# A two-layer hybrid decoder trunk on one core: the first projections in a written order, the levels of a triangular inverse ahead of their bank's readers, and one buffer taken later

## The chip, the core and the metric

The kernel runs on one core of a Trainium2 chip. The metric is device time in microseconds (us) of one execution, the median of three runs. TensorE (PE in the profile) multiplies matrices into PSUM banks of 128 partitions by 512 float32 values; VectorE (DVE), ScalarE (ACT) and GpSimd (POOL) do the rest, and all DMAs here are issued by SyncE (SP).

## The reference

Two pre-norm residual layers over 1,024 tokens of width 1,024, float32. Layer 0 has a gated DeltaNet and a short gated convolution side by side, layer 1 an HGRN2 recurrence and a dilated window attention; each layer ends with a SwiGLU feed-forward of 2,816 hidden columns. The parts that the change touches:

```python
hn = rms_norm(h, norm_mix_g[layer])
qkv, z, beta_raw, alpha_raw, gate_b, gate_c, sc_in = split_cols(h @ w_in, AB_SPLITS)
qkv = silu(causal_depthwise_conv(qkv, conv_w))          # width 4
...
# gated delta rule, chunks of tokens, one triangular solve per chunk and head
sol = triangular_solve(a_strict + eye(c), rhs, lower=True, unit_diagonal=True)
...
return (silu(h @ w_gate) * (h @ w_up)) @ w_down         # swiglu
```

## The kernel before

Tokens are held transposed: features on the partitions, tokens along the free dimension, in two halves of 512. A tile of x is 128 features by 512 tokens; there are 8 of them (d = 0 to 7) for each half. To keep float32 accuracy at the fast matmul rate, every operand is split into a rounded high part and the remainder (`split`, L97: a copy on ScalarE, L99, and a subtraction on VectorE, L100), and `mm3` (L120) makes each product of three matmuls: high by high (L123), low by high (L124) and high by low (L125). `proj` (L131) runs 8 such triples into one PSUM bank: 24 matmuls for 128 output columns and 512 tokens.

PSUM has three groups of banks: `psu` (3 buffers), `psm` (3) and `psg` (2). A new tile of a group waits for the readers of the tile that had the buffer before it.

Most of the program's order on each engine is made by a scheduler that looks at priorities and expected times. Inside `manual_schedule` the engines named keep the order in which the code records the work.

*The start.* x is loaded by SP together with the first four weights, `("ab", 0)`, `("ab", 4)`, `("ab", 8)`, `("ab", 12)` (query, key, value and gate of head 0; 512 KB each, two staging buffers `raw`). For each half and each d, ScalarE makes the high part of x times the gain (L1655), VectorE the low part (L1656), and `Trunk.piece` (L169) squares x on ScalarE and adds the squares up on VectorE (L183). `Trunk.rms` (L185) sums over the partitions with small matmuls (L195), VectorE adds epsilon (L198) and GpSimd takes the power (L200); `Trunk.spread` (L204) broadcasts the result over the partitions with matmuls (L209), and ScalarE copies it to `rb` (L1659). The projections are of the unscaled x: `rb` is multiplied in afterwards, where VectorE reads the bank (L781 in `conv_silu`, L721 in `z_gate`). All of this is left to the scheduler.

*Units.* `mixer_ab` goes through 8 units u: head h = u // 2 and half u % 2. A unit is four projections (query, key, value, gate), the convolution of width 4 over the first three (`conv_silu`: L781, L790, L792, then a Tanh on ScalarE and L796), and `z_gate`. Between them, `step` (L862) runs pieces of other work by the letters of `plan` (L858): S is a piece of `scalars` (beta and decay), A and B are the two parts of `chunk_mats` of earlier units.

*The inverse.* After a substitution on blocks of 32, `delta` builds the inverse of each chunk's 128 by 128 triangle in levels. `level1` and `level2` make the off-diagonal blocks of 32, `level3` and `level4` those of 64. Each level is a few small matmuls into a part of a `psg` bank, and then a read of it: level1 by VectorE (L975), level2 by VectorE (L990), level3 by ScalarE (L1002), level4 by VectorE (L1009). In one tick level4 of chunk c + 1 and level2 of chunk c + 2 share a bank, in the next one level3 and level1. TensorE's order here is written out: `short_conv`'s projections are cut in halves of 12 matmuls, and a tick of `delta` stands between them.

*The turn of the feed-forward.* `Up` multiplies with a Strassen-like scheme: the products are named p1 to p7, and `Up.turn` (L410) writes out the order for the first three weight columns while the second half's operands are made. `rest` (L463) makes low parts of operands (L413) from `tr.h`, the trunk's tiles; then `close()` frees these tiles, and the pool `self.right` is opened over their memory. `take` (L266) gives a weight buffer: the 9th and 10th taken are the first ones that lie in this pool. `p7` (L359) copies its bank out to `c` (L362, ScalarE), which for f = 0 is also a tile of this pool (`kept`, L349), and adds z to it (L363); `end` (L368) goes on accumulating into the same bank after that copy.

## Time and profile before

| | us |
|---|---|
| median of 3 runs (lowest to highest) | 2687.57 (2687.46 to 2688.88) |
| the profiled execution, by the same clock as the runs | 2687.8 |
| its span, from the first instruction to the last | 2686.0 |

The profiled execution thus has 1.8 us around its span, and lies 0.2 us above the median of the runs. Times in the trace count from the start of the span. In a row of the timeline stand start, duration, engine, line, operation, tiles and the number of instructions merged (x8); brackets give how long the engine had been idle before it, and what ended that. Matmuls overlap, so the start of one to the start of the next is less than the duration shown.

### The profile page before, as it was taken

The numbers are of one execution on the slowest core, as the hardware profiler recorded it, in microseconds if no ns is written. First come the engines' busy times: TensorE is split into PE (matmuls) and PEld (weight loads), VectorE is DVE, ScalarE is ACT, GpSimd is POOL, SyncE is SP. The second block draws the span as 40 slices with busy tenths as digits, with TensorE's granted clock in tenths as the row PEclk, the third lists the DMA queues.
The fourth block names the chain that finished last, engine by engine and source line by source line (L and its number), as shares of the span: only waits on it lengthen the run. The fifth ranks groups of instructions, "written<-read, shape, count | busy, mean of one in ns | idle before, by whom it ended". The sixth has DMA issues, their size and how long they took to land.

```text
span 2686.0 us, 36890 instructions
## 1 busy us (share of the span) xinstructions
PE 2654.1 (99%) x14604; PEld 2221.7 (83%) x14604; DVE 1479.6 (55%) x2463; ACT 986.0 (37%) x1623; POOL 480.4 (18%) x434
## 2 busy tenths in 40 slices
PE   8999999999999999999999999999999999999998
PEld 6888788878888888888888888888887888888887
DVE  7887676583434443345665557477658344444342
ACT  4432123343333332323444345354434333333232
POOL 0110121334333201010000000000034343320100
PEclk9999999999999999999999999999999999999999
DMA  3424346422222384441222322323742222237342
GB/s 131 141 96 165 108 140 208 146 75 90 84 81 81 99 274 129 154 131 52 79 67 73 87 64 68 99 64 123 241 147 75 91 86 81 91 101 262 114 137 94
DMA packets 166285, 310.65 MB, mean 116 GB/s; under 512 B 26048, under 2 KB 65504, under 8 KB 165984
## 3 DMA queue, kind: packets, MB, share of 16 engines
q1 hardware_dynamic: 166112, 308.30, 35.3%
q8 instruction: 114, 1.87, 0.3%
q14 instruction: 59, 0.48, 0.1%
HBM read 234.22 MB, written 74.01 MB: 115 GB/s over the span
## 4 chain that ended last, share of the span: by engine, by line
PE 94%; DVE 3%; issue 1%; DMA 1%; ACT 1%; POOL 0%; SPq 0%; POOLq 0%; DVEq 0%; ACTq 0%
PE psu L123 20%; PE psu L125 20%; PE psu L124 20%; PE psg L123 5%; PE psg L125 5%; PE psg L124 5%; PE psm L123 3%; PE psm L124 3%; PE psm L125 3%; PE psm L1487 1%; PE psm L1461 1%; PE psg L1250 1%; PE psm L195 1%; PE psm L1476 1%; DVE h L413 1%
## 5 line engine op out<-in xcount | busy, mean ns | idle before, releaser
L100 DVE TENSOR_TENSOR w<-raw,w 128x1024 fp32r<-128x1024 f32 (+1 forms) x324 | 404.8, 1251 | 442.5 <-ACT w L99 441.2
L99 ACT CAST w<-raw 128x1024 fp32r<-128x1024 f32 (+1 forms) x324 | 319.5, 987 | 635.2 <-PE psg L125 230.8
L123 PE MATMUL psu<-hnh,w 128*128 128x512 f32 x1328 | 530.2, 399 | 6.9 <-ACT w L99 6.9
L125 PE MATMUL psu<-hnh,w 128*128 128x512 f32 x1328 | 520.3, 392 | 0.0
L124 PE MATMUL psu<-hnl,w 128*128 128x512 f32 x1328 | 518.6, 391 | 0.0
L123 PEld LDWEIGHTS psu<-hnh,w 128*128 128x128 f32 x1328 | 250.7, 189 | 57.4 <-ACT w L99 6.9
L125 PEld LDWEIGHTS psu<-hnh,w 128*128 128x128 f32 x1328 | 250.1, 188 | 54.1 <-DVE w L100 0.8
L124 PEld LDWEIGHTS psu<-hnl,w 128*128 128x128 f32 x1328 | 250.6, 189 | 49.6 <-DVE hnl L1656 0.2
L183 POOL TENSOR_TENSOR acc<-acc,sq 128x512 f32<-128x512 f32 x48 | 73.0, 1520 | 531.2 <-ACT sq L179 426.3
L123 PE MATMUL psu<-hidq,w 128*128 128x512 f32 (+1 forms) x352 | 134.8, 383 | 0.0
L125 PE MATMUL psu<-hidq,w 128*128 128x512 f32 (+1 forms) x352 | 134.6, 382 | 0.0
L124 PE MATMUL psu<-hidq,w 128*128 128x512 f32 (+1 forms) x352 | 134.6, 382 | 0.0
L123 PE MATMUL psu<-w,hnh 128*128 128x512 f32 (+1 forms) x320 | 113.1, 353 | 0.0
L125 PE MATMUL psu<-w,hnl 128*128 128x512 f32 (+1 forms) x320 | 111.2, 347 | 0.0
L124 PE MATMUL psu<-w,hnh 128*128 128x512 f32 (+1 forms) x320 | 111.1, 347 | 0.0
L337 DVE TENSOR_TENSOR gt<-gt,psm 128x512 f32<-128x512 f32 x40 | 27.5, 688 | 145.2 <-PE psm L125 142.8
L379 POOL TENSOR_TENSOR hid<-hid,c 128x512 f32<-128x512 f32 x44 | 83.2, 1891 | 127.6 <-ACT hid L378 127.6
L305 POOL TENSOR_TENSOR raw<-raw,ws 128x512 f32<-128x512 f32 x38 | 51.4, 1354 | 281.8 <-DVE w L100 281.8
L1288 POOL COPY attn<-ac 32x128 f32<-32x128 f32 x32 | 13.4, 418 | 434.4 <-DVE ac L1254 381.6
L100 DVE TENSOR_TENSOR hidq<-hr,hidq 128x1024 fp32r<-128x1024 f32 x44 | 54.2, 1231 | 49.6 <-ACT hidq L99 48.9
L125 PEld LDWEIGHTS psu<-hidq,w 128*128 128x128 f32 x352 | 66.2, 188 | 12.9
L124 PEld LDWEIGHTS psu<-hidq,w 128*128 128x128 f32 x352 | 66.2, 188 | 12.9
(420 smaller groups left out, 5665.6 us busy)
## 6 DMA issues: line engine op xcount, KB each, us to landing
raw<-in_dram SPq DMA_DIRECT2D x274, 512.0 KB, 3.6
hid<-hid SPq DMA_DIRECT2D x88, 256.0 KB, 2.2
hr<-hid SPq DMA_DIRECT2D x44, 512.0 KB, 4.5
hd<-h SPq DMA_DIRECT2D x48, 256.0 KB, 2.7
h<-hd SPq DMA_DIRECT2D x48, 256.0 KB, 6.0
scr_c<-cx SPq DMA_DIRECT2D x8, 1216.0 KB, 5.1
h<-in_dram SPq DMA_DIRECT2D x32, 256.0 KB, 5.4
cxb<-scr_c SPq DMA_DIRECT2D x8, 1024.0 KB, 5.9
```

The costliest lines, as they stand in the source:

```text
L99: S.copy(hi, src)
L100: eng.tensor_tensor(lo, src, hi.bitcast(F32), op=SUB)
L123: T.matmul(o, lh, rh, start=first and i == 0, stop=False, **kw)
L124: T.matmul(o, lh, rl, start=False, stop=False, **kw)
L125: T.matmul(o, ll, rh, start=False, stop=last and i == n - 1, **kw)
L183: (eng or G).tensor_tensor(a, a, q, op=ADD)
L195: T.matmul(st[:, j:j + 1], x[:, j * P:(j + 1) * P], onesn, start=i + j == 0, stop=i == 1, skip_group_check=True)
L305: G.tensor_tensor(a[:, HT:], a[:, HT:], s[:, :HT], op=SUB)
L337: V.tensor_tensor(g, g, self.y.pop(f), op=ADD)
L379: G.tensor_tensor(h, h, self.c22.pop(f), op=MULT)
L413: eng.tensor_tensor(dst, x, y, op=SUB)
L1250: T.matmul(od[r * 32:(r + 1) * 32, c * 32:(c + 1) * 32], a[:, z], x[:, z], start=True, stop=True, tile_position=(0, r * 32))
```

## The change

Four things change.

1. The start is written out for TensorE, VectorE and ScalarE. The first half's high and low parts come first (`scaled_in`), the weights' splits at fixed places among them (`arrived`), then the squares. `mixer_ab` records the first unit's four projections itself: query, key, the partition sums of the first half's norm (`tr.rms(0)`), the first 12 matmuls of value, the broadcast (`tr.spread`), the other 12, and gate. The second half's parts are recorded in between by `second` (step 0 and 1: four tiles of x each, then its squares; step 2: its norm's sums; step 3: its broadcast and copy), with query and key of the second half ahead of step 2 and step 3. `lead` is what stood at the head of `conv_silu`.
2. `plan` moves the pieces of `scalars` and `chunk_mats` in units 1 and 2.
3. Every level yields between its matmuls and its read, and `levels` records the matmuls of both levels of a bank before the reads of both.
4. In `turn` the second of two weight buffers is taken after `p7(0)` and not before it; the pool's tiles lie at other places for that.

No instruction is added or removed on the engines that compute: TensorE, VectorE, ScalarE, GpSimd and SP have as many as before.

```diff
@@ -504,9 +504,10 @@
             rest(b22, b1)
             close()
             self.right = right("up")
-            us = [self.take(), self.take()]
+            us = [self.take()]
             self.first = [self.hidden()]
             self.p7(0, t3)
+            us.append(self.take())
             self.right.tile([P, 32], F32, name="pad")
             self.p7(1, t3)
             self.add11(1, g[1])
@@ -621,7 +622,7 @@
                 yield
 
 
-    def mixer_ab(hn, rb, hp, close):
+    def mixer_ab(hn, rb, hp, tr, first, second, close):
         scr_n = dr.tile([4, 32, 32, 32], F32, name="scr_n")
         scr_y = dr.tile([4, 32, 32, 32], F32, name="scr_y")
         scr_c = dr.tile([8, P, 4, CX], F32, name="scr_c")
@@ -636,6 +637,37 @@
         tri, dmask = masks[:, 0, :], masks[:, 1, :]
         ones = fp.tile([P, P], F32, name="ones")
         V.memset(ones, 1.0)
+
+
+        wqk, wvz = first
+
+        def lead(o, half, carry=None):
+
+            xp = fp.tile([P, 3 + HT], F32, tag="xp", name="xp", bufs=3)
+            if half == 0:
+                G.memset(xp[:, 0:3], 0.0)
+            else:
+                G.tensor_copy(xp[:, 0:3], carry)
+            V.tensor_tensor(xp[:, 3:], o, rb[half], op=MULT)
+            return xp
+
+        early = {}
+        os3 = [proj(wk(wqk, 0), hn[0]), proj(wk(wqk, 1), hn[0])]
+        r = tr.rms(0)
+        os3.append(proj(wk(wvz, 0), hn[0], range(KH), last=False))
+        pb = tr.spread(r)
+        proj(wk(wvz, 0), hn[0], range(KH, KT), os3[2], first=False)
+        second(0)
+        S.copy(rb[0], pb)
+        for which, o in enumerate(os3):
+            early[0, which] = lead(o, 0)
+        early[0, 3] = proj(wk(wvz, 1), hn[0])
+        second(1)
+        early[1, 0] = proj(wk(wqk, 0), hn[1])
+        second(2)
+        early[1, 1] = proj(wk(wqk, 1), hn[1])
+        second(3)
+        ordered.close()
         close()
         with ExitStack() as es:
             keep = hp
@@ -715,8 +747,8 @@
                     S.activation(sca["gt"], sca["gl"], AF.Exp)
 
 
-            def z_gate(h, half, w):
-                o = proj(w, hn[half])
+            def z_gate(h, half, w, o=None):
+                o = o or proj(w, hn[half])
                 sz = fil.tile([P, HT], F32, tag="zs", name="zs", bufs=2)
                 V.tensor_tensor(sz, o, rb[half], op=MULT)
                 th = fil.tile([P, HT], F32, tag="zt", name="zt", bufs=2)
@@ -772,13 +804,9 @@
                     return p.tile([P] + list(shape), F32, tag=tag, name=tag, bufs=bufs)
 
                 def conv_silu(h, which, w, half, carry, d):
-                    o = proj(w, hn[half])
-                    xp = at("xp", (3 + HT,), 3, fp)
-                    if half == 0:
-                        G.memset(xp[:, 0:3], 0.0)
-                    else:
-                        G.tensor_copy(xp[:, 0:3], carry[:, which, :])
-                    V.tensor_tensor(xp[:, 3:], o, rb[half], op=MULT)
+                    xp = early.pop((h * 2 + half, which), None) or proj(w, hn[half])
+                    if h or half:
+                        xp = lead(xp, half, carry[:, which, :])
                     if half == 0:
                         G.tensor_copy(carry[:, which, :], xp[:, HT:])
                     a = at("cacc", p=fp)
@@ -855,7 +883,7 @@
                     dma(scr_c[c0:c0 + 4, :, h, :].rearrange("c p e -> p c e"), cx)
 
 
-                plan = {1: "SSSA", 2: "ABxB"}
+                plan = {1: "xSSS", 2: "ABAB"}
                 units, sc_ = [], scalars()
                 waiting = {"A": [], "B": []}
 
@@ -883,7 +911,7 @@
                     step(u, 1)
                     conv_silu(h, 2, wk(wvz, 0), half, carry, v)
                     step(u, 2)
-                    z_gate(h, half, wk(wvz, 1))
+                    z_gate(h, half, wk(wvz, 1), early.pop((u, 3), None))
                     step(u, 3)
                     waiting["A"].append(chunk_mats(h, half, kk, v))
             def inverses():
@@ -970,6 +998,7 @@
                         for r in (0, 64):
                             T.matmul(lv[r:r + 32, h * 32:(h + 1) * 32], als[c][r + 32:r + 64, h, r:r + 32],
                                      yd[r + 32:r + 64, e0 + h, :], start=True, stop=True)
+                    yield
                     z1 = z1s[c] = bt("z1", [4, 32])
                     for r in (0, 64):
                         V.tensor_copy(z1[r:r + 32], lv[r:r + 32, 0:P].rearrange("p (h t) -> p h t", h=4))
@@ -986,6 +1015,7 @@
                         for r in (0, 64):
                             T.matmul(lv[r:r + 32, 256 + h * 32:256 + (h + 1) * 32], xd[r:r + 32, c * 4 + h, :],
                                      z1[r:r + 32, h, :], start=True, stop=True)
+                    yield
                     for r in (0, 64):
                         V.tensor_scalar(yt[r:r + 32, :, r + 32:r + 64],
                                         lv[r:r + 32, 256:256 + P].rearrange("p (h t) -> p h t", h=4),
@@ -998,6 +1028,7 @@
                     for h in range(4):
                         T.matmul(lv[0:64, 256 + h * 64:256 + (h + 1) * 64], al[64:128, h, 0:64],
                                  yt[64:128, h, 64:128], start=True, stop=True)
+                    yield
                     z2 = z2s[c] = bp.tile([64, 4, 64], F32, tag="z2", name="z2", bufs=1)
                     S.copy(z2, lv[0:64, 256:512].rearrange("p (h t) -> p h t", h=4))
                     load_al(c + 3)
@@ -1006,6 +1037,7 @@
                     yt, x64, z2 = yts[c % 2], x64s[c % 2], z2s.pop(c)
                     for h in range(4):
                         T.matmul(lv[0:64, h * 64:(h + 1) * 64], x64[:, h, :], z2[:, h, :], start=True, stop=True)
+                    yield
                     V.tensor_scalar(yt[0:64, :, 64:128], lv[0:64, 0:256].rearrange("p (h t) -> p h t", h=4),
                                     -1.0, None, op0=MULT)
                     if c:
@@ -1089,23 +1121,25 @@
                     V.scalar_tensor_tensor(go, v4(o), vec[:, R_DNG:R_DNG + 1], szc, op0=MULT, op1=MULT)
                     dma(catd[half][0:4, :, cc * P:(cc + 1) * P].rearrange("k p t -> p k t"), go)
 
+                def levels(*fs):
+
+                    fs = [(f, c) for f, c in fs if 0 <= c < 8]
+                    if fs:
+                        o = psg()
+                        gs = [f(c, o) for f, c in fs]
+                        for _ in range(2):
+                            for g in gs:
+                                next(g, None)
+
                 for c in range(-3, 8):
                     if c > -3:
                         if c >= 0:
                             values(c)
-                        la = psg() if c < 7 else None
-                        if 0 <= c + 1 < 8:
-                            level4(c + 1, la)
-                        if 0 <= c + 2 < 8:
-                            level2(c + 2, la)
+                        levels((level4, c + 1), (level2, c + 2))
                         yield
                     if 0 <= c < 7:
                         state(c)
-                    lb = psg() if c < 6 else None
-                    if 0 <= c + 2 < 8:
-                        level3(c + 2, lb)
-                    if 0 <= c + 3 < 8:
-                        level1(c + 3, lb)
+                    levels((level3, c + 2), (level1, c + 3))
                     if 1 <= c + 1 < 8:
                         level5(c + 1)
                     if c >= 0:
@@ -1635,28 +1669,67 @@
     hp = mes.enter_context(pool("mix"))
     dma(vec, vecs)
     tr.begin(0, x_t[0], (0,))
-    first = [wload(("ab", 0))]
+    hn = [[quarter(), quarter()] for _ in range(NH)]
+    rb = [hp.tile([P, HT], F32, name=f"rb{half}") for half in range(NH)]
+
+    def scaled_in(half, d):
+
+        x, g = tr.at(half, d), vec[:, R_MIX + d:R_MIX + d + 1]
+        hi, lo = hk(hn[half], 0, d), hk(hn[half], 1, d)
+        S.activation(hi, x, AF.Copy, scale=g)
+        V.scalar_tensor_tensor(lo, x, g, hi.bitcast(F32), op0=MULT, op1=SUB)
+
+    def second(step, r=[]):
+
+        if step < 2:
+            for d in range(KH * step, KH * step + KH):
+                scaled_in(1, d)
+            if step:
+                squares(1, range(KT))
+        elif step == 2:
+            r.append(tr.rms(1))
+        else:
+            S.copy(rb[1], tr.spread(r.pop()))
+
+    def coming(name):
+
+        u, raw = unit(), ring.tile([P, DM], F32, tag="raw", name="raw", bufs=2)
+        dma(raw, w_all[W_AT[name]])
+        return u, raw
+
+    def arrived(u, raw):
+        split(u[:, 0, :], u[:, 1, :], raw)
+        return u
+
+    def squares(half, ds):
+        for d in ds:
+            tr.piece(half, d, V)
+
+    E = mybir.EngineType
+    ordered = ExitStack()
+    ordered.enter_context(tc.manual_schedule(engines={E.PE, E.DVE, E.Activation}))
+    w0 = coming(("ab", 0))
     tr.load(0, x_t[0], range(1, 4))
-    first += [wload(("ab", 4))]
+    w1 = coming(("ab", 4))
     tr.load(0, x_t[0], range(4, KT))
     dma(cf[:, 0:P], c_f[:, 0:P])
-    first += [wload(("ab", 8)), wload(("ab", 12))]
+    scaled_in(0, 0)
+    first = [[arrived(*w0)], []]
+    for d in range(1, 4):
+        scaled_in(0, d)
+    first[0].append(arrived(*w1))
+    w0, w1 = coming(("ab", 8)), coming(("ab", 12))
     ring.tile([P, 24], F32, name="pad")
-    first = [first[0] + first[1], first[2] + first[3]]
     tr.begin(1, x_t[1])
     dma(cf[:, P:], c_f[:, P:C_TRI])
     dma(ci, c_i)
-    hn, rb = [], []
-    for half in range(NH):
-        hn.append([quarter(), quarter()])
-        for d in range(KT):
-            x, g = tr.at(half, d), vec[:, R_MIX + d:R_MIX + d + 1]
-            hi, lo = hk(hn[half], 0, d), hk(hn[half], 1, d)
-            S.activation(hi, x, AF.Copy, scale=g)
-            V.scalar_tensor_tensor(lo, x, g, hi.bitcast(F32), op0=MULT, op1=SUB)
-            tr.piece(half, d, V)
-        rb.append(hp.tile([P, HT], F32, name=f"rb{half}"))
-        S.copy(rb[half], tr.spread(tr.rms(half)))
+    for d in range(4, KT):
+        scaled_in(0, d)
+    squares(0, range(3))
+    first[1].append(arrived(*w0))
+    squares(0, range(3, 5))
+    first[1].append(arrived(*w1))
+    squares(0, range(5, KT))
     residual = x_t
 
     def finish(half, dg):
@@ -1682,7 +1755,7 @@
     for layer in range(2):
 
         if layer == 0:
-            mixer_ab(hn, rb, hp, es.close)
+            mixer_ab(hn, rb, hp, tr, first, second, es.close)
         else:
             dg1 = tr.rms(1)
             mes = ExitStack()
```

## The prediction

> **What bounds the kernel now.** I read the head of the page and its chain of waits first, then the list of what TensorE waited for, then windows around those waits, and last the timelines there.
>
> ```profile
> span 2686.0 us, 36890 instructions
> PE 2654.1 (99%) x14604; PEld 2221.7 (83%) x14604; DVE 1479.6 (55%) x2463; ACT 986.0 (37%) x1623; POOL 480.4 (18%) x434
> ...
> PE 94%; DVE 3%; issue 1%; DMA 1%; ACT 1%; POOL 0%; SPq 0%; POOLq 0%; DVEq 0%; ACTq 0%
> ```
>
> TensorE is busy for 99% of the span and makes 94% of the chain that ended last. The change leaves the number of instructions alone, so it can only win idle time of TensorE, or time in which TensorE runs slowly. The list of TensorE's waits (total, times, longest) shows how much there is:
>
> ```profile
> PE psu L123 <- ACT w L99: 6.9, 1, 6.9
> PE psu L123 <- ACT c L362: 5.1, 2, 2.5
> PE psg L987 <- DVE yt L1009: 4.1, 7, 1.0
> PE psg L971 <- ACT z L1002: 3.5, 7, 0.5
> PE psm L209 <- POOL r L200: 2.4, 2, 1.3
> PE psm L195 <- DVE acc L183: 1.0, 1, 1.0
> ```
>
> The first row is the wait for the first weight, which stays. The others are what the three parts of the change go for: the turn of the feed-forward (L362, once in each layer), the levels (L987, L971), and the norms in the start (L209, L195). They sum to 16.1 us. Windows (length; busy PE, PEld, DVE, ACT, POOL; granted clock) show a second loss behind an idle stretch:
>
> ```profile
> 32.20:35.50 3.30, 2.43 (x10) 2.34 (x11) 3.30 (x7) 0.32 (x1) 1.33 (x3) 0.50 0.00 0
> 60.00:300.00 240.00, 239.59 (x1127) 199.83 (x1126) 193.23 (x420) 74.67 (x216) 23.47 (x49) 1.00 0.40 130
> 571.50:574.90 3.40, 0.88 (x4) 0.47 (x3) 2.67 (x3) 1.14 (x3) 0.00 (x0) 1.00 0.00 0
> 574.90:578.30 3.40, 3.40 (x9) 2.65 (x9) 1.82 (x4) 3.39 (x5) 0.00 (x0) 0.50 0.00 0
> ```
>
> After the idle stretch at 571.5 the granted clock is 0.50 for 3.4 us, although TensorE is fully busy again: half of that, 1.7 us, is lost on top. From 60 to 300 us TensorE is idle for 0.4 us in all; what is won ahead of it arrives at the levels, if VectorE (193 of 240 us busy) keeps up.
>
> **The start.** TensorE's timeline before:
>
> ```profile
> 6.94 0.79 PE L123 MATMUL psu<-hnh,w 128*128 128x512 f32 x1 [6.94 <-ACT w L99]
> ...
> 12.44 0.39 PE L125 MATMUL psu<-hnh,w 128*128 128x512 f32 x1
> ...
> 22.24 1.05 PE L209 MATMUL psm<-cf,r 128*128 128x128 f32 x8
> 23.05 0.48 PE L125 MATMUL psu<-hnh,w 128*128 128x512 f32 x1
> ...
> 23.60 0.39 PE L125 MATMUL psu<-hnh,w 128*128 128x512 f32 x1
> ...
> 28.38 0.39 PE L125 MATMUL psu<-hnh,w 128*128 128x512 f32 x1
> 29.77 1.05 PE L195 MATMUL psm<-onesn,acc 128*128 128x1 f32 x8 [1.00 <-DVE acc L183]
> ...
> 33.07 2.08 PE L209 MATMUL psm<-cf,r 128*128 128x128 f32 x8 [1.35 <-POOL r L200]
> 34.79 0.77 PE L123 MATMUL psu<-hnh,w 128*128 128x512 f32 x1
> ...
> 39.10 0.40 PE L124 MATMUL psu<-hnl,w 128*128 128x512 f32 x1
> ```
>
> From 23.60 to 28.38 stand 21 matmuls, 0.228 us each. What is lost: 28.61 to 29.77, 1.16 us, where the three `psu` banks are full and the sums of the second half wait for VectorE; 1.35 us for GpSimd's power; 0.91 us because the broadcast L209 takes 1.72 us (33.07 to 34.79) at the low clock and 0.81 at the high one (22.24 to 23.05); 2.03 us because the ten matmuls from 34.79 to 39.10 take 4.31 us and not 2.28. Sum 5.45 us. In the written order both norms stand between projections: each broadcast has 12 or 24 matmuls (2.7 or 5.5 us) between it and its sums, which cover the 1.35 us and the rest of GpSimd's way, and the gate's projection finds its bank free, since VectorE reads the query's bank right after the first broadcast.
>
> New waits come where the order gets ahead of ScalarE and VectorE. Their rows:
>
> ```profile
> 10.01 1.05 ACT L99 CAST w<-raw 128x1024 fp32r<-128x1024 f32 x1
> 23.33 0.59 ACT L1659 COPY rb<-psm 128x512 f32<-128x512 f32 x1 [1.76 <-PE psm L209]
> ...
> 11.26 1.22 DVE L100 TENSOR_TENSOR w<-raw,w 128x1024 fp32r<-128x1024 f32 x1
> 13.00 0.74 DVE L1656 SCALAR_TENSOR_TENSOR hnl<-h,vec,hnh 128x512 fp32r<-128x512 f32 x1
> 13.66 0.68 DVE L183 TENSOR_TENSOR acc<-acc,sq 128x512 f32<-128x512 f32 x1
> 31.98 1.28 DVE L781 TENSOR_TENSOR xp<-psu,rb 128x512 f32<-128x512 f32 x2
> 33.18 0.87 DVE L790 TENSOR_SCALAR cacc<-xp,vec 128x512 f32<-128x512 f32 x2
> 33.97 4.06 DVE L792 SCALAR_TENSOR_TENSOR cacc<-xp,vec,cacc 128x512 f32<-128x512 f32 x6
> ```
>
> First, the fifth tile of x: its low part stands on VectorE behind the second weight's subtraction. The weight's cast ends at 11.06, the subtraction (1.22) at 12.28, the low part (0.74) at 13.0. TensorE's 14th matmul needs it and before started at 12.44, so it waits 0.55. After that a low part comes every 0.66 us (13.00 to 13.66) and three matmuls take 0.68. Second, the first norm's sums: matmuls 14 to 48 bring TensorE to 21.0; VectorE has four low parts (2.6), six additions (4.1) and two weights' subtractions (2.4) from 12.3, which end at 21.4: 0.4 us. Third, the second norm's sums: TensorE gets there after sums (1.95), 72 matmuls (16.4) and a broadcast (0.81), at 40.6. VectorE can begin at 27.5, after the first broadcast (26.9) and its copy (0.59), and has two and one `xp` (1.9), two first taps (0.9), four low parts (2.6), six additions (4.1), four further taps (2.7) and one product with `cth`, taken as 0.68: 12.9 us, to 40.4, so no wait, or one of a few tenths. Every one of these tiles that is late holds up what stands behind it: on VectorE the convolution, on ScalarE the Tanh, and neither is needed by TensorE before the transposes of unit 0 some 30 us on.
>
> I take 0.95 us of new waits: **4.5 us won**. The bounds: 5.45 if the new waits vanish, 2 if each is a microsecond longer. On SP the first 32 issues stand in the same order; the staged weight that waits for the second subtraction leaves at 12.3, where that subtraction ended at 12.48 before, and the second half of x behind it is no later. GpSimd gets nothing new ahead of its powers. The moved pieces of `plan` I take as nothing: TensorE's work fills those stretches (0.4 us idle from 60 to 300), and without that cover they cost or give those 0.4.
>
> **The levels.** A tick before, with its wait, and one at the end of `delta` in which L971 no longer follows:
>
> ```profile
> 375.55 0.68 PE L999 MATMUL psg<-yt,al 64*64 64x64 f32 x8
> 376.73 0.44 PE L971 MATMUL psg<-yd,al 32*32 32x32 f32 x16 [0.51 <-ACT z L1002]
> ...
> 406.58 0.67 PE L999 MATMUL psg<-yt,al 64*64 64x64 f32 x8
> 407.19 1.16 PE L1021 MATMUL psg<-y,cxb 128*128 128x128 f32 x8
> ```
>
> L971 does not read what ScalarE copies; it waits since it writes the same bank. Recorded ahead of the copy it follows L999 directly: 0.61 us after its start instead of 1.18, 0.57 us less. There are 14 such waits in the list; 14 by 0.57 is 8.0, and the longest (1.0) has 0.46 more: **8.4 us won**, at least the 7.6 us of idle time. In return the reads start later, by the 0.44 of L971 or L987; what reads `z` and `yt` on TensorE comes one tick later, behind 12 matmuls (2.7 us), so this stays hidden.
>
> **The turn.** TensorE, ScalarE, VectorE:
>
> ```profile
> 571.47 0.39 PE L125 MATMUL psu<-t3h,w 128*128 128x512 f32 x1
> 574.39 0.50 PE L123 MATMUL psu<-t4h,w 128*128 128x512 f32 x1 [2.52 <-ACT c L362]
> ...
> 573.75 1.07 ACT L362 COPY c<-psu 128x512 f32<-128x512 f32 x2 [3.16 <-DVE b22l L413]
> ...
> 568.94 2.43 DVE L413 TENSOR_TENSOR t4l<-h,t4h 128x1024 fp32r<-128x1024 f32 x2
> 571.28 2.35 DVE L413 TENSOR_TENSOR b22l<-h,b22h 128x1024 fp32r<-128x1024 f32 x2
> ```
>
> The copy's data are in PSUM long before 573.75; it waits for `b22l`, which still reads the trunk's memory under `c`. With the second weight buffer taken later, `c` lies over another trunk tile, whose last reader is `t4l`, as the waits of the built program show, and the weight buffer gets the late place; it is written only after `b22l` in any case. The copy then starts at 571.41 and TensorE 0.64 us later, as in the rows above (573.75 to 574.39): at 572.05, where 571.70 is the earliest. 2.34 us won, and with so short a gap the 1.7 us at half clock too (L971's 0.51 leaves it at 1.00): 4.04, **8.1 us in both layers**. Next late is VectorE's addition to `c` behind `b22l`, about 574.3, which TensorE needs at 574.8. If the clock fell all the same, 4.7.
>
> [...]
>
> **Sum.** 4.5 + 8.4 + 8.1 = 21.0 us. The profiled execution took 2687.8 us (span 2686.0 and 1.8 around it), which gives 2666.8; it stands 0.2 above the median of the runs, so I say 2666.6.
>
> **Rivals.**
> - *The start gives nothing* (0.10): VectorE, full from 32.2 to 35.5 before, is late for both norms and the clock falls once or twice at 1.7 us. For it: my two sums of VectorE's work end within half a microsecond of TensorE. Against it: they are full durations, and the rows overlap by 0.08. 2666.6 + 4.5: 2671.1.
> - *The wait of the levels moves* (0.07): the change does not do what it says, since the bank's guard remains and the later reads are waited for at the next tick. For it: seven of the waits are for VectorE, which in 60 to 300 us is at 80%. Against it: 2.7 us of cover. 2675.0. [...]
> - *The clock stays low in the turns* (0.05), being tied to something other than the gap: 2666.6 + 3.4 = 2670.0. Against it: also the window at 32.2, again behind idle time. [...]
> - *Slower* (0.03): the second half's low parts, queued on VectorE behind `xp` and so behind the first broadcast, stop TensorE in the query's second projection. It decides from parts that come 21 us later than TensorE asks for them (about 34.9 us; I have them at 33.5), so past 56 us; at 62 us the time is 2693. VectorE's work does not reach that far.
> - Unnamed shortfalls of 2 to 20 us: 0.05, of which 0.02 lie within 5.4 us of the time before.
>
> **How the numbers follow.** The forecast has 0.70, and its own bounds are 2665 (all idle gone: 5.45 in the start, 8.4, and 2 by 4.4 in the turns, the whole 2.69 and 1.7 of each) and 2670 (2 + 7.6 + 8.1). The first two rivals pull the upper end of the range to 2674; I put the lower at 2663. This kernel can be told from no change beyond about 0.2%, 5.4 us: all cases but the slower one and those 0.02 lie below 2682: 0.70 + 0.10 + 0.07 + 0.05 + 0.03 make faster 0.95, same 0.02, slower 0.03.
>
> **What would show it.** In the new trace: no rows L987 and L971 among TensorE's waits; the wait on L362 at 0.4 or less, with clock 1.00 behind both turns; no window with clock 0.50 between 12 us and the end's last microseconds; waits on low parts and additions of at most a microsecond each before 45 us. A clock of 0.50 near 15, 25 or 42 us, or a new TensorE wait in `values` or `state`, would make the prediction wrong.

## The result, and the profile after

| | us | ratio to before, 95% interval |
|---|---|---|
| before, 4 runs | 2688.07 (2687.46 to 2688.88) | |
| changed, 4 runs | 2673.97 (2673.39 to 2675.34) | 0.9947 (0.9932 to 0.9963) |
| changed, 5 further runs beside other kernels | 2671.97 (2671.70 to 2674.18) | 0.9939 (0.9927 to 0.9952) |

The change wins 14.1 us in the first set and 16.4 in the second (2688.39 before there); over all nine runs of the changed kernel the median is 2673.4. The forecast was 21.0 won and a time of 2666.6; the range ended at 2674.0. So the direction and the three mechanisms are right, and 6.9 us of the gain, a third, are missing in the first set (4.6 in the second). This is the head of the page of the changed kernel, and the list of what TensorE waited for (total, times, longest):

```profile
span 2671.9 us, 36879 instructions
PE 2649.4 (99%) x14604; PEld 2216.8 (83%) x14604; DVE 1478.3 (55%) x2463; ACT 986.2 (37%) x1623; POOL 481.9 (18%) x434
```

```profile
PE psu L123 <- ACT w L99: 7.6, 1, 7.6
PE psu L123 <- ACT u L357: 2.6, 2, 1.4
PE psm L209 <- POOL r L200: 1.1, 1, 1.1
PE psm L880 <- DVE nn L872: 1.1, 5, 0.3
...
PE psg L123 <- DVE hid L377: 0.7, 1, 0.7
...
PE psu L123 <- ACT c L362: 0.5, 2, 0.3
```

The waits of the levels (7.6 us before) are gone, and `c` has fallen from 5.1 to 0.5. The `L209` row that is left is the one at the end of the kernel. New are `u` (2.6), `L880` (1.1), `L1117` (0.7), and a `hid` that has grown from 0.2 to 0.7. The timeline of TensorE in the changed kernel shows each part at work:

```profile
21.24 0.39 PE L125 MATMUL psu<-hnh,w 128*128 128x512 f32 x1
21.74 1.05 PE L195 MATMUL psm<-onesn,acc 128*128 128x1 f32 x8
...
101.69 0.48 PE L123 MATMUL psu<-hnh,w 128*128 128x512 f32 x1
...
309.64 0.68 PE L1029 MATMUL psg<-yt,al 64*64 64x64 f32 x8
310.25 0.44 PE L999 MATMUL psg<-yd,al 32*32 32x32 f32 x16
...
420.26 0.38 PE L1091 MATMUL psm<-st,cxb 128*128 128x128 f32 x2
...
561.54 0.39 PE L125 MATMUL psu<-t3h,w 128*128 128x512 f32 x1
562.16 0.50 PE L123 MATMUL psu<-t4h,w 128*128 128x512 f32 x1 [0.23 <-ACT c L362]
...
592.00 0.39 PE L125 MATMUL psg<-t1h,w 128*128 128x512 f32 x1
593.81 0.50 PE L123 MATMUL psu<-t3h,w 128*128 128x512 f32 x1 [1.42 <-ACT u L357]
...
2033.07 0.39 PE L125 MATMUL psu<-t3h,w 128*128 128x512 f32 x1
...
2063.55 0.39 PE L125 MATMUL psg<-t1h,w 128*128 128x512 f32 x1
2065.08 0.50 PE L123 MATMUL psu<-t3h,w 128*128 128x512 f32 x1 [1.14 <-ACT u L357]
```

The same matmuls stand in the timeline of before at these times (571.47 is in the prediction):

```profile
103.69 0.48 PE L123 MATMUL psu<-hnh,w 128*128 128x512 f32 x1
...
430.74 0.38 PE L1059 MATMUL psm<-st,cxb 128*128 128x128 f32 x2
...
605.81 0.39 PE L125 MATMUL psg<-t1h,w 128*128 128x512 f32 x1
606.04 0.39 PE L123 MATMUL psu<-t3h,w 128*128 128x512 f32 x1
...
2045.05 0.39 PE L125 MATMUL psu<-t3h,w 128*128 128x512 f32 x1
...
2079.41 0.39 PE L125 MATMUL psg<-t1h,w 128*128 128x512 f32 x1
2079.64 0.39 PE L123 MATMUL psu<-t3h,w 128*128 128x512 f32 x1
```

(The page's head counts 11 instructions fewer than before; these are semaphore instructions, and the counts of the engines' own work in its second line are the same.) Subtracting the times of the two kernels gives the lead of the changed one at each place. Behind the start it is 103.69 - 101.69 = 2.00 us. Behind the levels it is 430.74 - 420.26 = 10.48, so the levels gave 8.5; an L999 now starts 0.61 behind its L1029. Ahead of the first turn it is 571.47 - 561.54 = 9.93, and 30 us behind it 605.81 - 592.00 = 13.81, so the turn won 3.88. At the next matmul it is 606.04 - 593.81 = 12.23: 1.58 are lost at once, in the wait for `u`. In the second layer the same three leads are 11.98, 15.86 and 14.56: 3.88 won, 1.30 lost. Windows of the changed kernel (length; busy PE, PEld, DVE, ACT, POOL; granted clock) show that the clock did stay up behind the turn:

```profile
558.78:562.19 3.41, 3.18 (x15) 2.29 (x14) 3.41 (x4) 2.20 (x4) 0.00 (x0) 1.00 0.50 154
562.19:565.60 3.41, 3.41 (x15) 2.83 (x16) 3.31 (x5) 2.39 (x4) 0.00 (x0) 1.00 0.00 0
```

### The profile page after: what moved, and what is told of

It reads as the page before. It is cut to its first block, busy times and chain, and to the rows that moved or that the text cites. A ratio compares the mean times of both kernels' runs of the same rounds, so it can differ in the third digit from the quotient of the medians.

```text
span 2671.9 us, 36879 instructions
## 1 busy us (share of the span) xinstructions
PE 2649.4 (99%) x14604; PEld 2216.8 (83%) x14604; DVE 1478.3 (55%) x2463; ACT 986.2 (37%) x1623; POOL 481.9 (18%) x434
## 3 DMA queue, kind: packets, MB, share of 16 engines
q8 instruction: 114, 1.87, 0.3%
## 4 chain that ended last, share of the span: by engine, by line
PE 90%; DVE 5%; issue 2%; DMA 1%; ACT 1%; POOL 1%; SPq 0%; POOLq 0%; DVEq 0%; ACTq 0%
PE psu L123 20%; PE psu L125 19%; PE psu L124 19%; PE psg L123 5%; PE psg L125 5%; PE psg L124 5%; PE psm L125 3%; PE psm L123 3%; PE psm L124 3%; PE psm L1521 1%; PE psm L1495 1%; PE psg L1284 1%; PE psm L195 1%; PE psm L1510 1%; DMA raw<-in_dram 1%
## 5 line engine op out<-in xcount | busy, mean ns | idle before, releaser
L100 DVE TENSOR_TENSOR w<-raw,w 128x1024 fp32r<-128x1024 f32 (+1 forms) x324 | 404.8, 1251 | 441.4 <-ACT w L99 440.5
L183 POOL TENSOR_TENSOR acc<-acc,sq 128x512 f32<-128x512 f32 x48 | 73.3, 1527 | 531.9 <-ACT sq L179 427.4
L379 POOL TENSOR_TENSOR hid<-hid,c 128x512 f32<-128x512 f32 x44 | 84.7, 1926 | 124.7 <-ACT hid L378 124.7
L305 POOL TENSOR_TENSOR raw<-raw,ws 128x512 f32<-128x512 f32 x38 | 51.3, 1350 | 275.8 <-DVE w L100 275.8
L100 DVE TENSOR_TENSOR hidq<-hr,hidq 128x1024 fp32r<-128x1024 f32 x44 | 54.2, 1232 | 50.5 <-ACT hidq L99 49.8
L124 PEld LDWEIGHTS psu<-hidq,w 128*128 128x128 f32 x352 | 66.2, 188 | 12.9
L125 PEld LDWEIGHTS psu<-hidq,w 128*128 128x128 f32 x352 | 66.2, 188 | 12.9
```

Of the source, the lines that this page charges most:

```text
L100: eng.tensor_tensor(lo, src, hi.bitcast(F32), op=SUB)
L124: T.matmul(o, lh, rl, start=False, stop=False, **kw)
L125: T.matmul(o, ll, rh, start=False, stop=last and i == n - 1, **kw)
L183: (eng or G).tensor_tensor(a, a, q, op=ADD)
L305: G.tensor_tensor(a[:, HT:], a[:, HT:], s[:, :HT], op=SUB)
L379: G.tensor_tensor(h, h, self.c22.pop(f), op=MULT)
```

## The experiments

All are edits of the changed kernel, five runs each (seven of levels_back, eleven of rest_pool), in three sets, each beside runs of before on the same chip. Medians of before in the three sets are 2687.62, 2688.39 and 2688.67. The first set asks where the two missing pieces went: the start (2.0 for 4.5) and the turn.

**The table of steps as before.**

```diff
-                plan = {1: "xSSS", 2: "ABAB"}
+                plan = {1: "SSSA", 2: "ABxB"}
```

> The changed kernel with the table of fill-in steps as before (SSSA, ABxB in place of xSSS, ABAB); the start, the levels and the turn stay changed. Theory P: the start as such won what it should, and about 2.1 us of it went into the transposes L880 near 85 and 101 us, which come one projection behind the products L867 and find VectorE not done; with two projections between them again the row L880 <- DVE nn leaves TensorE's waits, and the time is 2674.0 - 2.1 = 2671.9 us. Rival S: the start itself won less, because the first weight came 0.6 us later and the clock rose later; the table is worth nothing: 2674.0, within 0.5.

Measured: 2672.78 us, ratio 0.9942 (0.9930 to 0.9955). The wait L880 is gone as theory P said, but another has come in its place, in TensorE's waits of this kernel:

```profile
PE psg L867 <- DVE cx L872: 1.2, 1, 1.2
```

The second A of the old table stands one projection behind the first, and with the new start VectorE has not read the first one's `psg` bank by then, as it had in before. The new table does cost time, but the old one is no longer its cure; the time, 2672.78, lies between theory P's and rival S's and decides nothing.

**Two projections between A and B.**

```diff
-                plan = {1: "xSSS", 2: "ABAB"}
+                plan = {1: "xSSS", 2: "AABB"}
```

> The changed kernel with AABB in place of ABAB for the third unit, nothing else. Theory P: two projections stand between each A and its B, so the wait L880 <- DVE nn goes (1.1 us in the list, 2.1 us of pitch): 2671.9 us. Rival Q: not the distance counts but that VectorE is full there; then the wait stays or moves to the second group of transposes L834, and the time is 2674.0 or above.

> AABB alone once more, beside the two: 2670.6 within 1 us, with the waits for u (2.3 us in two) as before.

Measured: 2670.63 us, ratio 0.9935 (0.9923 to 0.9948), and in the third set 2670.06, ratio 0.9931 (0.9918 to 0.9945): 2.8 and 3.3 us under the 2673.4 of the changed kernel, whose runs stand in other sets; the traces, below, are the surer measure. Theory P holds: the row `L880` is gone and none has come for `L834`, so rival Q falls. These are the first two of four transposes near 85 us in the changed kernel's timeline; near 101 us two more of them wait in the same way:

```profile
85.01 0.33 PE L880 MATMUL psm<-cf,nn 128*128 128x128 f32 x1 [0.31 <-DVE nn L872]
85.53 0.33 PE L880 MATMUL psm<-cf,nn 128*128 128x128 f32 x1 [0.19 <-DVE nn L872]
```

And with AABB, in the timeline of `plan_aabb`:

```profile
99.03 0.60 PE L880 MATMUL psm<-cf,nn 128*128 128x128 f32 x4
99.39 0.48 PE L123 MATMUL psu<-hnh,w 128*128 128x512 f32 x1
```

A transpose which waits takes 0.52 to the next, where four in a row take 0.36 in all (99.03 to 99.39). So the 1.1 us of idle time in the list is less than what is lost, about 2 us. At 99.39 the lead over before is 103.69 - 99.39 = 4.30 us, where the changed kernel has 2.00. Of these 2.3 us 0.2 come from the start itself: the two kernels are alike up to the first products L867, and begin them at 77.11 and 77.33, although their first weights came at 6.89 and 7.56. So the table cost 2.1 us, and the late first weight of rival S next to nothing.

**The buffers taken as before.**

```diff
-            us = [self.take()]
+            us = [self.take(), self.take()]
             self.first = [self.hidden()]
             self.p7(0, t3)
-            us.append(self.take())
```

> The changed kernel with both weight buffers taken ahead of p7(0), as before. Theory V: each turn loses 2.3 us of idle time and 1.5 us at half clock again, but the wait for u behind it (1.4 and 1.3 us) goes, since TensorE comes later: 2674.0 + 7.6 - 2.7 = 2678.9 us. As forecast, without a return: 2674.0 + 8.1 = 2682.1 us.

Measured: 2677.30 us (2674.87 to 2677.70), ratio 0.9957 (0.9944 to 0.9971), 3.9 above the 2673.4 of the changed kernel. That is nearer to theory V's 4.9 than to the 8.1 of the forecast, and 1.6 us below theory V's 2678.9. Its list of TensorE's waits has `c` back and no row for `u`:

```profile
PE psu L123 <- ACT c L362: 5.4, 3, 2.6
```

So the wait for `u` belongs to the turn's own gain: a TensorE that comes some 4 us later finds `u` copied.

**Less for VectorE in the turn.** What makes `u` late? The chain behind the turn, followed backwards in the timelines of the changed kernel:

```profile
593.19 0.57 ACT L357 COPY u<-psu 128x512 f32<-128x512 f32 x1
...
587.98 1.05 ACT L99 CAST w<-ws 128x1024 fp32r<-128x1024 f32 x1 [6.67 <-POOL ws L291]
...
586.66 1.29 POOL L291 TENSOR_TENSOR ws<-ws,raw 128x512 f32<-128x512 f32 x1 [3.04 <-DMA raw<-in_dram]
...
582.35 1.55 SPq L263 DMA_DIRECT2D raw<-in_dram  x2
...
572.02 1.55 POOL L379 TENSOR_TENSOR hid<-hid,c 128x512 f32<-128x512 f32 x1 [19.77 <-ACT hid L378]
```

And the last of these rows in the kernel before:

```profile
583.19 1.54 POOL L379 TENSOR_TENSOR hid<-hid,c 128x512 f32<-128x512 f32 x1 [21.00 <-ACT hid L378]
```

The copy `u` stands on ScalarE behind casts of weights. Their sum on GpSimd waits for a load, and that load leaves SP right behind a store that waits for GpSimd's second product L379. GpSimd begins on its series at 572.02, when VectorE has come through the turn. That is 11.17 us earlier than before, and the load leaves 11.17 earlier too (593.52 before), the copy `u` 11.61 (604.80 before); TensorE is 13.81 ahead at this place. So the chain had lost its share when GpSimd began. In before, `u` was done 0.67 us ahead of TensorE (604.80 + 0.57 to 606.04), and 13.81 - 11.61 - 0.67 is 1.5, about the 1.58 that TensorE lost. So the first idea was to take work from VectorE:

```diff
             sub(G, u2[:, :HT], w2[:, :HT], u2[:, :HT])
+            for c in (lo, hi): sub(G, b22[1][:, c, :], b1[:, c, :], b22[0][:, c, :].bitcast(F32))
...
             rest(t4, b0)
-            rest(b22, b1)
```

> The changed kernel with the two subtractions for b22l in the turn on GpSimd, which is idle there for 20 us, instead of VectorE; they are recorded ahead of p6(0). Theory V: behind the turn TensorE is bound by a chain that begins on VectorE (b22l, c, hid), goes over GpSimd's product to SP's store, to the weight loads queued behind it, and ends in ScalarE's copy u; with 2.4 us less on VectorE the wait L123 <- ACT u L357 (2.6 us in two) goes, and the wait on c (0.5) too: 2674.0 - 3.0 = 2671.0 us. Rival D: the weight loads themselves are late (4.2 us from issue to landing) and do not move: 2674.0. Rival G: GpSimd needs 4.4 us for each subtraction beside VectorE, b22l comes late for the product s4, and it is slower than 2674.5.

Measured: 2685.75 us (2682.04 to 2687.83), ratio 0.9991 (0.9982 to 1.0000): nearly all of the change's gain is lost. Theory V falls. The time is on rival G's side, but not for its reason: what comes late first is not `b22l` but `t3l`, which stayed on VectorE. VectorE, GpSimd and TensorE in the timeline of this kernel:

```profile
554.93 6.75 DVE L413 TENSOR_TENSOR t3l<-h,t3h 128x1024 fp32r<-128x1024 f32 x2
...
553.89 6.71 POOL L413 TENSOR_TENSOR b22l<-h,b22h 128x1024 fp32r<-128x1024 f32 x2
...
561.74 0.51 PE L124 MATMUL psu<-t3l,w 128*128 128x512 f32 x1 [1.66 <-DVE t3l L413]
```

The same two subtractions for `t3l` take 2.42 in the changed kernel, where GpSimd is idle. Side by side the four fill the 7.79 us from 553.89 to 561.68, and VectorE's end 1.08 after GpSimd's (560.60). One after the other they would need 7.6 us by an estimate: VectorE's 2.42, and 5.2 for GpSimd's four half tiles at the 1.28 and 1.30 that its L291 and L301 take in the changed kernel from 574.90 on, where VectorE is idle. So the two engines as good as took turns here. `t3l` is not all of the loss: by the lead over before, TensorE loses 3.0 us ahead of the turn in each layer, wins 2.6 in it and not 3.9, and loses 2.3 and 2.4 in the wait for `u`, whose row has grown to 4.4 in two.

**The store off SP's queue.** The second idea was the link on SP.

```diff
-            dma(self.hid[1, f], h)
+            (G.dma_start if f < 2 else dma)(self.hid[1, f], h)
```

> The changed kernel with the two stores of hid's second half in the turn issued from GpSimd's own queue instead of SP's; nothing of the computation moves. Theory V, its link on SP: behind the turn the next weight load leaves at 582.35 only because it stands behind the store that waits for GpSimd's product (581.92), while its buffer is free at 580.76; it now leaves 1.5 us earlier, and with it GpSimd's sum, ScalarE's casts and copy u, and the wait L123 <- ACT u L357 (1.4 and 1.2 us) goes: 2674.0 - 2.6 = 2671.4 us. Rival D: the store is no link, the time from issue to landing sets it: 2674.0. [...]

> The edit of store_pool and AABB in the table of steps together. If both causes are what they are taken for, they add up: 2674.0 - 3.3 (as AABB alone measured) - 2.6 = 2668.1 us; if the store is no link, 2670.6 as with AABB alone.

Measured: 2673.08 us, ratio 0.9942 (0.9929 to 0.9954), and with AABB 2670.89, ratio 0.9934 (0.9921 to 0.9948). Neither is clearly below the kernel that it was made from, so the time fits rival D, and 2668.1 is missed by 2.8. GpSimd's two issues take 0.76 and 0.58 us in the timeline. The list of TensorE's waits tells more than the time: the row for `u` is gone and one for `c` has come, 10 us earlier.

```profile
PE psg L123 <- DVE c L363: 1.8, 2, 0.9
```

Its cause, in the timeline of `store_pool`, with the load that was to leave earlier:

```profile
577.09 3.73 DVE L100 TENSOR_TENSOR w<-ws,w 128x1024 fp32r<-128x1024 f32 x1 [3.89 <-ACT w L99]
...
577.17 1.31 POOL L305 TENSOR_TENSOR raw<-raw,ws 128x512 f32<-128x512 f32 x1
578.42 1.30 POOL L379 TENSOR_TENSOR hid<-hid,c 128x512 f32<-128x512 f32 x1
...
581.98 2.02 SPq L263 DMA_DIRECT2D raw<-in_dram  x2
```

The subtraction for `w`, 1.22 us when alone, takes 3.73: it contains the two GpSimd products whole (1.22 + 1.31 + 1.30 = 3.83). In the changed kernel the subtraction keeps its 1.22, and it is GpSimd's L305 and L379 that take 2.29 and 2.28. Theory V falls with that. The load no longer stands behind the store, but its buffer, which VectorE reads after the long subtraction, is free only at 581.96, and not at 580.76; as this kernel is 0.88 us further ahead at the turn, the load leaves 0.5 later by that measure. The copy `u` ends at 592.77, by the same measure 0.1 earlier. The row for `u` is gone because TensorE, held up by `c`, comes later. So taking the store away does not bring `u` forward: behind it stand VectorE and GpSimd, which held each other up in these rows (3.73 for 1.22, 2.29 for 1.31).

**Sums back from GpSimd to VectorE.** If the two engines run as one, the sum of their times counts, and a half tile costs 1.30 us on GpSimd (L301 at 576.14 in the changed kernel) and 0.68 on VectorE (L183 at 13.66 in before). So the third idea is the opposite of the first. `w3` moves all four half-tile sums of the first weight unit behind the turn (f = 3), and `sum3` only the two for `ws`:

```diff
-    def sums(self, a, b):
+    def sums(self, a, b, eng=G):
...
-            G.tensor_tensor(s[:, HT:], b[:, :HT], b[:, HT:], op=ADD)
-            G.tensor_tensor(s[:, :HT], s[:, HT:], a[:, :HT], op=SUB)
+            eng.tensor_tensor(s[:, HT:], b[:, :HT], b[:, HT:], op=ADD)
+            eng.tensor_tensor(s[:, :HT], s[:, HT:], a[:, :HT], op=SUB)
...
-            s = self.sums(a, b)
+            s = self.sums(a, b, V if f == 3 else G)
```

(`w3` has the same `V if f == 3 else G` in L301 and L305 as well.)

> The changed kernel with the four half-tile sums for the first weight unit behind the turn (ws twice, raw twice, unit 3) on VectorE instead of GpSimd. Theory L: VectorE's additions and subtractions of two tiles in SBUF and GpSimd's exclude each other (the subtraction for w took 3.73 us with two GpSimd products beside it, and 1.22 alone), so behind the turn the two run as one engine, and TensorE is bound by their sum; on VectorE such a half tile costs 0.68 against GpSimd's 1.3, so the chain gets some 2.5 us shorter, the wait L123 <- ACT u L357 goes and none comes in its place: 2673.4 (all runs of the changed kernel) - 2.4 = 2671.0 us. Rival V: VectorE alone sets the pace; it has 2.7 us more to do, and TensorE waits longer for c or u: 2674.5 or above.

> The edit of w3 and AABB in the table of steps together: by theory L 2670.6 - 2.4 = 2668.2 us, the lowest so far; by rival V 2672 or above.

> As w3_aabb, but only the first two of the four sums (ws) on VectorE, where VectorE was idle for 3.2 us anyway. Theory L: the cast of ws comes 1.8 us earlier, about the 1.4 us that TensorE waited; 2668.2 to 2669.5 us. Rival V: 2670.6 or above.

| | us | ratio to before, 95% interval |
|---|---|---|
| w3 | 2670.43 (2669.20 to 2672.22) | 0.9934 (0.9921 to 0.9946) |
| w3 with AABB | 2668.50 (2667.08 to 2669.99) | 0.9925 (0.9913 to 0.9938) |
| sum3 with AABB | 2667.64 (2666.45 to 2669.53) | 0.9923 (0.9911 to 0.9936) |
| AABB alone, same set | 2670.06 (2669.29 to 2670.52) | 0.9931 (0.9918 to 0.9945) |

The times are theory L's in all three (sum3 with AABB lies 0.6 below its range), and rival V falls: VectorE has more to do, and TensorE waits less. The row for `u` is gone from TensorE's waits, with none in its place. These rows are all that is left of the feed-forward's own in the list for sum3 with AABB, beside the one for L277 that before has too:

```profile
PE psu L123 <- ACT c L362: 0.6, 2, 0.3
PE psg L123 <- DVE hid L377: 0.2, 1, 0.2
```

It beats both kernels of this study: 21.0 us under before in the same set (2688.67), 5.8 under the changed kernel's 2673.4. Moving two sums is as good as moving four. What these runs show is that the two sums stand in the chain to `u`: ahead of the turn sum3 with AABB is as far ahead of before as `plan_aabb` (12.9 us), and behind it the load leaves at 577.64 instead of 579.38 and `u` ends at 589.26 instead of 590.83. They do not separate the two reasons for it: VectorE needs less time for such a sum (1.18 and 0.69 us for L290 and L291 in `w3`, against 1.29 and 1.28 on GpSimd in the changed kernel), and GpSimd's work then stands in VectorE's way less.

**The levels as before.** `levels` and the four yields were undone:

```diff
-                        levels((level4, c + 1), (level2, c + 2))
+                        la = psg() if c < 7 else None
+                        if 0 <= c + 1 < 8:
+                            level4(c + 1, la)
+                        if 0 <= c + 2 < 8:
+                            level2(c + 2, la)
...
```

> The changed kernel with the levels of the triangular inverse recorded as before (each level's copy straight behind its matmuls, one level after the other); the start and the turn stay. As forecast: the 14 waits L971 <- ACT z and L987 <- DVE yt come back and cost 8.4 us: 2682.4. Theory R, part of it had been given back later (the wait L1117 <- DVE dgo of 0.7 us, which only the changed kernel shows): 2681.7 or less.

Measured: 2681.16 us (2679.47 to 2682.22), ratio 0.9972 (0.9961 to 0.9982). That is 7.8 above the 2673.4 of the changed kernel and 9.2 above its median in the same set, so both 8.4 and a little less fit; the two theories are too near each other for these times. The timelines speak for the forecast: the changed kernel's second profile leads this one by 9.2 us behind the levels and by some 9.4 at the end, so nothing was given back. The waits are back, in this kernel's list:

```profile
PE psg L1016 <- DVE yt L1041: 4.1, 7, 1.0
PE psg L999 <- ACT z L1033: 3.6, 7, 0.5
```

**The changed kernel once more.**

> The changed kernel once more, beside the others. If the late first weight (7.6 us against 6.9) belongs to the new order of the start, it is 7.6 again; if it is the loads' own scatter, it lies anywhere in 6.7 to 8.1, as in the experiments with the same start so far, and the time within 2 us of 2674.0. Theory W on the clock: it falls for one window of 3.41 us behind a window in which TensorE streamed wide tiles for less than about 1.5 us, the one-column sums counting as idle; so the sums of the norms can cost a window, if they lie in one window together with idle time.

Measured: 2671.97 us, as in the first table. That is 2.0 below 2674.0, at the edge of what was expected. The first weight's wait is 7.4 us here, 6.7 to 8.1 in the thirteen profiled runs with this start, and 6.9 in the one of before: the loads' scatter is enough to explain 7.6, and nothing points at the new order. The wait L1117 of 0.7 us is in one profile of the changed kernel, but not in the other and in none of the edited kernels, so it is no steady cost of the change.

## Why the prediction was right, and where the missing third went

| part | forecast | first profile of the changed kernel |
|---|---|---|
| start with the table of steps | 4.5 | 2.0 (4.3 with AABB) |
| levels | 8.4 | 8.5 |
| turns | 8.1 | 7.8 won, 2.9 lost again behind them: 4.9 |
| sum | 21.0 | 15.4, less 1.3 in small losses elsewhere: 14.1 |

**The number.** The 2673.97 us of the first set lie 0.03 inside the range of 2663 to 2674, but outside the forecast's own bounds of 2665 and 2670, as do the second set's 2671.97. The upper end had been pulled up for two rivals that did not occur. That the range held is luck; what was right are the three mechanisms, and two terms of the sum fell short.

**The bound.** Right: the number of instructions did not change, and all of the gain is idle time of TensorE or time at half clock. (Of the 16.1 us of waits that the prediction added up, 1.1 belong to the `L209` at the end of the kernel, which no part of the change touches; the forecast does not use that sum.)

**The start.** The 5.45 us of loss came back about as worked out, and the 0.95 of new waits was more than there was in the first profile: the sums start 0.27 late (21.24 + 0.23 to 21.74). The low part of the fifth tile, taken at 0.55, did not show there: the clock rose later (13.26 us, against 11.67), and up to it TensorE's matmuls start 0.43 us apart, behind it 0.23, so TensorE came to that tile later. In `store_pool` and `w3` the wait is there, 0.6 and 0.8. With AABB the lead behind the start is 4.30. The step that failed is "The moved pieces of `plan` I take as nothing: TensorE's work fills those stretches". The 0.4 us of idle time was read off the old order. The new table puts B one projection (5.5 us) behind its A, and VectorE needs longer than that for what lies between: the products of an A begin at 77.33, and VectorE's last read for `nn` begins at 86.16, some 9 us later. It cost 2.1 us, which `plan_aabb` gives back. The lower bound of 2 for the start does not follow from its own sum: two new waits a microsecond longer leave 2.5, three 1.5.

**The levels.** Right in mechanism and size: 0.61 from L1029 to L999, where before had 1.18 from L999 to L971; 8.5 in sum over the 14 waits; and the later reads stayed hidden, but for the 0.7 at `L1117` in one of two profiles.

**The turn.** Right as far as it was followed: the wait for `c` is 0.23 (forecast 0.35), the clock stayed at 1.00, and 3.88 us are won in each turn (forecast 4.04). The step that failed is "next late is VectorE's addition to `c` behind `b22l`, about 574.3, which TensorE needs at 574.8". That addition did come in time, but the prediction stopped there. VectorE is full there (3.41 and 3.31 of 3.41 us in the two windows above), so what hangs on its work could not move forward with TensorE: GpSimd's products, the loads on SP behind their store, the casts, and the copy `u`, which TensorE needs 32 us on. GpSimd's first product came only 11.17 us earlier than before, and in the first layer TensorE kept 12.23 of its 13.81 us of lead. `take_back` shows that the wait hangs on the turn's gain, `w3` and `sum3` that GpSimd's two sums stand in the chain, and the rows of `rest_pool` and `store_pool` that VectorE and GpSimd held each other up (6.75 us for 2.42, 3.73 for 1.22).

**The rivals.** None of the named ones is the case; the time lies among the shortfalls that the prediction had no name for. "The clock stays low" and "the wait of the levels moves" are refuted by the rows above.

**The signs.** Those named for the levels, for `c`, for the clock behind the turns and for small waits in the start came out as said in the changed kernel's two profiles, but for the clock's first rise, which came at 13.26 us in the first of them and not by 12. One sign of being wrong, a clock of 0.50 near 25 us, is in `rest_pool` (23.79 to 27.20 us) and in `w3` (24.57 to 27.99), though not in the changed kernel's first profile (1.00 from 23.50 to 26.91); the prediction had no term for it, and the last section has what ran ahead of it.

## What to carry to other kernels

When a wait in front of the bounding engine is taken away, ask of every chain that runs beside it, and not only of the next reader, whether it moves along; one that hangs on another engine's unbroken work moves only as far as that work has gaps, and beyond that its old slack is all that can be won. Idle time read from the old order prices nothing that the edit moves: count the distance between producer and consumer in the new order. Ahead of moving work between VectorE and GpSimd, look at the durations of either beside the other.

## What the runs showed of the hardware that was not expected

**VectorE and GpSimd held each other up.** Two VectorE subtractions of 128x1024 take 2.42 us in the changed kernel, with GpSimd idle, and 6.75 in `rest_pool` beside two of GpSimd's; one takes 1.22 with GpSimd idle (L100 at 11.26 in before) and 3.73 in `store_pool` beside two GpSimd products of half the size. In the second case the GpSimd products keep their 1.3 us each, and the subtraction takes about its own time and theirs; in the first the four take 7.79 in all, where 7.6 is the estimate for one after the other.

**The partition sums went with the low clock.** In before, the granted clock is 0.50 behind each turn for 3.41 us, from 574.87 to 578.28 and from 2049.43 to 2052.84. In windows of that length, busy time of TensorE, and the part of it that is the sums L195 (128x1, given by the same view for that line alone), in `w3` and then in `store_pool`:

```profile
21.16:24.57 3.41, 3.18 (x22) 2.81 (x22) 1.51 (x5) 2.70 (x5) 0.75 (x1) 1.00 1.07 395
24.57:27.99 3.42, 3.42 (x10) 2.70 (x10) 1.83 (x3) 0.00 (x0) 0.71 (x1) 0.50 0.29 115
...
21.16:24.57 3.41, 1.95 (x16) 1.86 (x16) 1.00 1.07 395
```

```profile
21.52:24.93 3.41, 3.41 (x23) 3.13 (x24) 1.51 (x5) 2.19 (x4) 1.26 (x1) 1.00 1.05 377
24.93:28.35 3.42, 3.42 (x20) 2.96 (x19) 1.87 (x3) 1.18 (x3) 0.20 (x1) 1.00 0.14 56
...
21.52:24.93 3.41, 1.87 (x16) 1.78 (x16) 1.00 1.05 377
```

Without the sums, `w3` has 3.18 - 1.95 = 1.23 us in its window and falls to 0.50 for the next; `store_pool` has 3.41 - 1.87 = 1.54 and stays at 1.00. Idle time alone does not tell them apart: it is 0.23 us in `w3`'s window, and the changed kernel's window at 558.78, further up, has the same 3.18 us without such sums and is followed by 1.00. Laid end to end from the clock's first rise (11.67 us in before, 13.26 in the changed kernel), these are the windows at 1.00 in the two traces that 0.50 follows, with two that 1.00 follows (the others of the two traces have 1.57 us or more), and one of `rest_pool`:

| | busy TensorE without L195, us | granted clock in the next 3.41 us |
|---|---|---|
| before, 28.74 to 32.15 | 1.98 - 1.95 = 0.03 | 0.50 |
| changed, 2661.99 to 2665.41 | 1.64 - 0.93 = 0.71 | 0.50 |
| before, 571.46 to 574.87 | 0.89 | 0.50 |
| `rest_pool`, 20.37 to 23.79 | 3.25 - 1.95 = 1.30 | 0.50 |
| before, 2674.07 to 2677.48 | 2.47 - 1.11 = 1.36 | 0.50 |
| before, 2046.02 to 2049.43 | 1.46 | 0.50 |
| changed, 20.08 to 23.50 | 3.31 - 1.76 = 1.55 | 1.00 |
| changed, 40.56 to 43.97 | 3.41 - 1.84 = 1.57 | 1.00 |

This fits theory W, as an estimate from these windows alone: less than about 1.5 us of other work in a window went with half clock in the next one, which costs 1.7 us. Windows that begin at 0.50 are apart: before has 2.49 us from 32.15 to 35.56, and 0.50 again up to 38.98. `rest_pool` and `w3` lost 1.7 us behind the first norm's sums; the changed kernel's first profile, with 1.55 us there, did not.
